# Down projection of the feed-forward stage by one level of Strassen's method over pairs of tiles, with weight sums and running sums on GpSimd

## The chip, the core and the metric

The kernel runs on one core of a Trainium2 chip. The metric is the device time of one execution in microseconds. Engines are named as in the profile: PE (TensorE), DVE (VectorE), ACT (ScalarE), POOL (GpSimd), SP (the engine that issues the DMAs).

## The reference, cut to what matters

One step of a two-layer encoder on 512 prompt frames and 8 × 16 sample frames. Each layer ends with a gated feed-forward stage, which is where the change lies:

```python
def swiglu(h, w_gu, w_down):
    g, u = jnp.split(h @ w_gu, 2, axis=-1)
    return (jax.nn.silu(g) * u) @ w_down
...
x = x + swiglu(rmsnorm(x, g_ffn[i]), w_ffn_gu[i], w_ffn_down[i])
```

The width is 1024 and the hidden width 2816, which is 22 tiles of 128. The 640 rows (512 prompt, 128 sample) are five tiles.

## The kernel before, in words

All products are float32 in three passes: a factor is held as a high part (rounded to the format that PE takes) and a low part (the rest), and hi·hi, hi·lo and lo·hi are added up in PSUM. So each weight goes through a **split**: ACT rounds it into `whi`, and DVE subtracts, `wlo = raw - whi`, with both inputs in SBUF (L1090, L1091 in `split_pair`). There are three buffers each of `whi` and `wlo`, 1024 columns wide.

The feed-forward stage works on pairs of hidden tiles, `g` = 0 to 10. `gate_up(g)` makes the gate and then the up projection, each by Winograd's form of Strassen's method: seven products of 12 matmuls over 320 columns, where plain products would need eight. For them `weights` forms four sums of weight blocks (`tw`, L1105 to L1108, one buffer, on DVE), and DVE adds each product from PSUM into results (L1133). `up` multiplies with the gate (L1170), and `finish` splits the activations into `aT` (L1055 on ACT, L1056 on DVE), in four pieces of 320 columns as they come.

`down` is plain before the change: after the gate of every even `g`, the two finished pairs g-2 and g-1 are multiplied with their rows of the down weight: 10 outputs of 128 rows by 512 columns, 12 matmuls of 512 columns each, and each is added from PSUM to the residual `X` by `add_x` (L318, DVE). So one **period** of the stage, over two pairs, holds two gates, two ups and one down. Each layer has five periods; the pair g = 10 is left for a last down, tile by tile, before the next norm.

The order of each engine's instructions is fixed when the program is built, by a scheduler that starts from the order in the code. Each engine works through its own list in order. Five PSUM banks serve these products (three `mm`, two `ps_s`).

Of the kernel before, what the change touches and what calls it, by code (L numbers as in the profile page):

```python
# [18 lines left out]
P = 128  # L19
# [73 lines left out]
def fox_mla_kernel(ctx: ExitStack, tc: tile.TileContext, I, O):  # L93
# [906 lines left out]
    def ffn_phase(l, nx, rest, g_next, cls=None):  # L1000
# [4 lines left out]

        w_gu, w_dn = I["w_ffn_gu"][l], I["w_ffn_down"][l]
# [3 lines left out]
        H0, H1 = slice(0, HALF), slice(HALF, NT)  # L1010
        with tc.tile_pool(name=f"ffn{l}", bufs=2, reuse_waits="tile") as fp:
# [33 lines left out]
            def alloc(g):  # L1045
                t = fp.tile([P, 2, 2, NT], F32R, tag="big", name="aT", bufs=2)
                aTs[g] = [t[:, 0], t[:, 1]]
# [4 lines left out]
            def finish(g, j, r):  # L1052

                a, (hi, lo) = avs[g], aTs[g]
                A.copy(hi[:, j, r], a[:, j, r])  # L1055
                V.tensor_tensor(lo[:, j, r], a[:, j, r], hi[:, j, r].bitcast(F32), ALU.subtract)  # L1056

            def plain(g):
# [3 lines left out]
                for n in range(2):  # L1062
# [6 lines left out]
                    def done(ps, j, hs, n=n):  # L1069
                        if n == 0:  # L1070
                            A.activation(a[:, j, hs], ps[:, 0:HALF], AF.Silu)
                        else:
                            V.tensor_tensor(a[:, j, hs], ps[:, 0:HALF], a[:, j, hs], ALU.mult)
                            finish(g, j, hs)
# [7 lines left out]
                return [lambda: alloc(g)] + L  # L1082
# [12 lines left out]
            def weights(c0):  # L1095
# [24 lines left out]
            def winograd(c0, out):  # L1120
# [19 lines left out]
                def p6(ps):  # L1140
                    d["u2"] = add(tmp("u2"), ps, "p1")
# [7 lines left out]
                def p5(ps):  # L1149
                    out(1, H1, add(tmp("c", 2), ps, "u3"))  # L1150
                    d["u4"] = add(tmp("u4"), ps, "u2")
# [11 lines left out]
            def gate_up(g):  # L1163
                a = avs[g] = a_tile()

                def gate(j, r, src):
                    A.activation(a[:, j, r], src, AF.Silu)

                def up(j, r, src):
                    V.tensor_tensor(a[:, j, r], src, a[:, j, r], ALU.mult)  # L1170
                    finish(g, j, r)

                return winograd(g * P, gate), [lambda: alloc(g)] + winograd(DFF + g * P, up)

            def down(gs):
# [3 lines left out]
                def load(half, g):  # L1179
# [3 lines left out]
                    d[half, g] = split_pair((raw, 2 * W))  # L1183

                def tile_half(t, half):
                    ac = slice(t * P, (t + 1) * P)

                    def ops():
                        return [(aTs[g][ai][:, j, ac], d[half, g][j][wi]) for g in gs for j in range(2) for wi, ai in PASSES]
                    return gemm(ops, 512, lambda ps: add_x(t, half, ps))  # L1190

                return load, tile_half

# [7 lines left out]
            for g in range(1, NG):  # L1201
                gate, up = gate_up(g)
                run(gate)
                if g % 2 == 0:
                    load, tile_half = down([g - 2, g - 1])
                    for half in range(2):
                        load(half, g - 2)
                        load(half, g - 1)
                        for t in range(TT):
                            run(tile_half(t, half))  # L1210
                run(up)
            load, tile_half = down([NG - 1])
            load(0, NG - 1)
            load(1, NG - 1)
# [523 lines left out]
```

## Time and profile before

| | us |
|---|---|
| runs: median of 3 | 2128.96 |
| runs: lowest, highest | 2126.95, 2131.17 |
| profiled execution, its own time | 2136.22 |
| span of the profile (first to last instruction) | 2134.4 |
| PE busy | 2071.8 |
| DVE busy | 1394.1 |
| ACT busy | 900.2 |
| POOL busy | 176.0 |

The profile is one execution, 7.26 us above the median of the runs; 1.8 us of its time lie outside the span. Busy time is a union over the whole span, so a low share does not say that an engine is idle in every stage.

### The profile page before, as it was taken

Reading aid. Unit: us, or ns where it says so; the run is one execution under the profiler, and the core shown is the slowest. Engines: PE = TensorE matmul, PEld = TensorE weight load, DVE = VectorE, ACT = ScalarE, POOL = GpSimd, SP = SyncE. Lnnn points to the kernel's source line nnn. Section 1 sums busy time; section 2 is a strip of 40 time slices with the busy share of each in tenths; the row PEclk is TensorE's granted clock in tenths of the full one; section 3 lists DMA queues with packets and bytes.
Section 4 is the critical chain, followed back from the end, with each engine's and each line's share of the span. In section 5 each row is a group of like instructions: output and inputs, shape, how many; then the busy total and the mean of one; then the engine's idle time right before and its main releaser. Section 6 shows DMA issues by size and latency. Waiting matters only on the chain. (4 is left out here: it accounts for less than half of the span.)

```text
span 2134.4 us, 35883 instructions
## 1 busy us (share of the span) xinstructions
PE 2071.8 (97%) x14189; PEld 1863.8 (87%) x14189; DVE 1394.1 (65%) x2695; ACT 900.2 (42%) x1793; POOL 176.0 (8%) x362
## 2 busy tenths in 40 slices
PE   7999999999999999999999999999999999999998
PEld 7988888888987799999998878887887799999997
DVE  4454555554546796696687567767546796686686
ACT  4444444454443443343344455554443443343342
POOL 1221212120100000000002201100000000000000
PEclk9999999999999999999999999999999999999999
DMA  7443434477545322232222221112445322322221
GB/s 222 130 137 108 140 108 128 149 233 226 161 142 184 96 73 80 89 90 79 80 80 59 84 92 39 52 50 87 141 145 182 99 70 79 89 87 77 84 80 59
DMA packets 279280, 234.34 MB, mean 110 GB/s; under 512 B 15669, under 2 KB 255925, under 8 KB 279113
## 3 DMA queue, kind: packets, MB, share of 16 engines
q1 hardware_dynamic: 279112, 232.05, 35.6%
q8 instruction: 112, 1.84, 0.4%
q14 instruction: 56, 0.45, 0.1%
HBM read 214.80 MB, written 17.21 MB: 109 GB/s over the span
## 5 line engine op out<-in xcount | busy, mean ns | idle before, releaser
L204 PE MATMUL mm<-hT,whi 128*128 128x320 f32 x1744 | 293.1, 314 | 4.3 <-ACT hT L222 4.3
L204 PEld LDWEIGHTS mm<-hT,whi 128*128 128x128 f32 x1744 | 262.6, 189 | 12.0 <-ACT hT L222 5.7
L318 DVE TENSOR_TENSOR X<-mm,X 128x512 f32<-128x512 f32 x270 | 182.8, 687 | 118.2 <-PE mm L204 116.7
L151 DVE TENSOR_TENSOR wlo<-raw,whi 128x1024 fp32r<-128x1024 f32 (+4 forms) x145 | 170.2, 1176 | 137.0 <-ACT whi L150 102.7
L150 ACT CAST whi<-raw 128x1024 fp32r<-128x1024 f32 (+4 forms) x145 | 144.7, 1002 | 162.5 <-PE mm L204 105.8
L204 PE MATMUL mm<-whi,oT 128*128 128x512 f32 x544 | 184.4, 411 | 1.3 <-DVE X L318 0.7
L1090 ACT CAST whi<-tw 128x512 fp32r<-128x512 f32 (+1 forms) x120 | 91.9, 766 | 213.0 <-PE mm L204 127.2
L204 PE MATMUL mm<-whi,aT 128*128 128x512 f32 x560 | 173.0, 390 | 0.3 <-ACT aT L1055 0.3
L204 PE MATMUL mm<-hT,wlo 128*128 128x320 f32 x872 | 156.7, 312 | 0.0
L204 PEld LDWEIGHTS mm<-hT,wlo 128*128 128x128 f32 x872 | 133.3, 188 | 3.2 <-issue 3.1
L204 PE MATMUL mm<-whi,hT 128*128 128x256 f32 (+2 forms) x800 | 127.5, 298 | 5.0 <-ACT whi L150 4.0
L204 PE MATMUL mm<-s,whi 128*128 128x320 f32 x768 | 128.2, 309 | 0.0
L204 PEld LDWEIGHTS mm<-whi,aT 128*128 128x128 f32 x560 | 104.4, 188 | 22.4 <-ACT aT L1055 1.1
L232 POOL TENSOR_SCALAR rstd<-ss 128x1 f32<-128x1 f32 x49 | 16.6, 339 | 1282.3 <-ACT hn L230 1277.8
L204 PEld LDWEIGHTS mm<-whi,hT 128*128 128x128 f32 x800 | 110.0, 193 | 10.3 <-ACT whi L150 4.5
L204 PEld LDWEIGHTS mm<-whi,oT 128*128 128x128 f32 x544 | 97.5, 190 | 22.7 <-issue 3.7
L204 PEld LDWEIGHTS mm<-s,whi 128*128 128x128 f32 x768 | 116.6, 188 | 0.0
L1091 DVE TENSOR_TENSOR wlo<-tw,whi 128x512 fp32r<-128x512 f32 (+1 forms) x120 | 103.5, 863 | 18.9 <-ACT whi L1090 16.7
L204 PE MATMUL mm<-wlo,oT 128*128 128x512 f32 x272 | 109.2, 402 | 0.0
L204 PE MATMUL mm<-wlo,aT 128*128 128x512 f32 x280 | 108.8, 389 | 0.0
L1090 ACT CAST whi<-raw 128x1024 fp32r<-128x1024 f32 x44 | 46.3, 1052 | 131.8 <-PE mm L204 72.3
L204 PE MATMUL ps_s<-whi,aT 128*128 128x512 f32 x320 | 98.6, 389 | 0.0
(340 smaller groups left out, 4289.0 us busy)
## 6 DMA issues: line engine op xcount, KB each, us to landing
rawg<-w_ffn_gu SPq DMA_DIRECT2D x80, 512.0 KB
raw<-w_ffn_down SPq DMA_DIRECT2D x44, 512.0 KB
raw<-w_x_kv SPq DMA_DIRECT2D x32, 512.0 KB
kr<-cache_mem_k SPq DMA_DIRECT2D x64, 256.0 KB
vr<-cache_mem_v SPq DMA_DIRECT2D x32, 512.0 KB
raw<-w_fox_in SPq DMA_DIRECT2D x30, 512.0 KB
kr<-cache_fox_k SPq DMA_DIRECT2D x16, 512.0 KB
vr<-cache_fox_v SPq DMA_DIRECT2D x16, 512.0 KB
```

The costliest lines, as they stand in the source:

```text
L150: A.copy(hi[:, 0:m], raw[:, 0:m])
L151: V.tensor_tensor(lo[:, 0:m], raw[:, 0:m], hi[:, 0:m].bitcast(F32), ALU.subtract)
L204: T.matmul(st["ps"][:, 0:n], lhsT=l, rhs=r, start=(j == 0), stop=(j == m - 1))
L232: G.tensor_scalar(r, ss, EPS, None, ALU.add)
L318: V.tensor_tensor(xs, ps, xs, ALU.add)
L1090: A.copy(hi[:, o:o + m], src)
L1091: V.tensor_tensor(lo[:, o:o + m], src, hi[:, o:o + m].bitcast(F32), ALU.subtract)
```

## The change

The four prompt tiles of the down projection become a Winograd product too (`down_winograd`): rows in two halves, columns in two halves, hidden tiles g-2 and g-1 as the blocks' inner parts. Seven products of 2 × 6 matmuls replace eight of the same size; the sample tile stays plain. `finish` runs once at the end of `up` and, except for the last pair, also forms and splits three sums of activations (256 columns each). The four sums of down-weight blocks (1024 columns) are taken on GpSimd in place in the loaded buffers, and all eight blocks are split, where four splits did before. Products that go into several outputs are first gathered in `u`, and GpSimd adds `u` to `X` (`spread`); the others are added by `add_x`. The four sums `tw` in `weights` go from DVE to GpSimd.

```diff
-                V.tensor_tensor(t[:, 2], b12, b11, ALU.subtract)
-                V.tensor_tensor(t[:, 0], b22, t[:, 2], ALU.subtract)
-                V.tensor_tensor(t[:, 1], b22, b12, ALU.subtract)
-                V.tensor_tensor(t[:, 3], b21, t[:, 0], ALU.subtract)
+                G.tensor_tensor(t[:, 2], b12, b11, ALU.subtract)
+                G.tensor_tensor(t[:, 0], b22, t[:, 2], ALU.subtract)
+                G.tensor_tensor(t[:, 1], b22, b12, ALU.subtract)
+                G.tensor_tensor(t[:, 3], b21, t[:, 0], ALU.subtract)
...
-            def finish(g, j, r):
-
-                a, (hi, lo) = avs[g], aTs[g]
-                A.copy(hi[:, j, r], a[:, j, r])
-                V.tensor_tensor(lo[:, j, r], a[:, j, r], hi[:, j, r].bitcast(F32), ALU.subtract)
+            def finish(g):
...
+                def split(c, src):
+                    A.copy(t[:, 0, c], src)
+                    V.tensor_tensor(t[:, 1, c], src, t[:, 0, c].bitcast(F32), ALU.subtract)
+
+                if g < NG - 1:
+                    a11, a12, a21, a22 = a[:, 0, R0], a[:, 1, R0], a[:, 0, R1], a[:, 1, R1]
+                    st = fp.tile([P, 3, NP // 2], F32, tag="u", name="st", bufs=2)
+                    V.tensor_tensor(st[:, 0], a21, a22, ALU.add)
+                    V.tensor_tensor(st[:, 1], st[:, 0], a11, ALU.subtract)
+                    V.tensor_tensor(st[:, 2], a12, st[:, 1], ALU.subtract)
+                    V.tensor_tensor(a21, a11, a21, ALU.subtract)
+                split(slice(0, M), a.rearrange("p j n -> p (j n)"))
+                if g < NG - 1:
+                    split(slice(M, M + 3 * NP // 2), st.rearrange("p j n -> p (j n)"))
...
+            def down_winograd(g0):
...
+                def sub(dst, x, y):
+                    G.tensor_tensor(d[dst], d[x], d[y], ALU.subtract)
...
+                def spread(i, *at):
+                    for r, half in at:
+                        G.tensor_tensor(xs(r, half, i), u[i], xs(r, half, i), ALU.add)
+
+                def p1(ps, i):
+                    u[i] = fp.tile([P, 512], F32, tag="u", name="u", bufs=2)
+                    A.copy(u[i], ps)
+                    spread(i, (0, 0))
+
+                def p6(ps, i):
+                    V.tensor_tensor(u[i], ps, u[i], ALU.add)
+                    spread(i, (0, 1))
+
+                def p7(ps, i):
+                    V.tensor_tensor(u[i], ps, u[i], ALU.add)
+                    spread(i, (1, 0), (1, 1))
...
+                def s1():
+                    split("b11", 0, 0)
+                    sub((0, 0), (0, 1), (0, 0))
+                    split("b21", 1, 0)
+                    both("b11", "11", p1)
+                    product("b11", 0, "s", 0, stop=False)
+
+                def s2():
+                    split("t1", 0, 0)
+                    sub((0, 0), (1, 1), (0, 0))
+                    sub((1, 0), (1, 0), (0, 0))
+                    product("b21", 1, "s", 0, start=False)
+                    add_x(TT - 1, 0, acc["s", 0])
+                    both("b21", "12", into((0, 0)))
+
+                def s3():
+                    split("b12", 0, 1)
+                    sub((0, 1), (1, 1), (0, 1))
+                    both("t1", "s1", into((0, 1), (1, 1)))
+
+                def s4():
+                    split("t2", 0, 0)
+                    product("b12", 0, "s", 0, stop=False)
+
+                def s5():
+                    split("b22", 1, 1)
+                    product("b22", 1, "s", 0, start=False)
+                    add_x(TT - 1, 1, acc["s", 0])
+                    both("b22", "s4", into((0, 1)))
...
+                def s8():
+                    both("t4", "22", into((1, 0)))
```

**POOL's list around a down.** Before, POOL has nothing to do in the whole feed-forward stage of layer 0 between one sum at its start (`s31`) and the small steps of the norm at its end (`rstd`):

```order
L232 TENSOR_SCALAR rstd_8811<-ss_8809 128x1
L233 TENSOR_TENSOR rstd_8811<-rstd_8811,mhalf_82 128x1
L1029 TENSOR_TENSOR s31_8933<-stmp_8930,s30_8932 128x1280
L232 TENSOR_SCALAR rstd_12830<-ss_12828 128x1
L233 TENSOR_TENSOR rstd_12830<-rstd_12830,mhalf_82 128x1
L232 TENSOR_SCALAR rstd_12853<-ss_12851 128x1
```

After, this stands in POOL's list around the first down of layer 0. `tw` are the sums for an up projection, `raw` and `rawd` the loaded down weights, `u` the two gathered products (9562 for the first tile of a row half, 9572 for the second):

```order
L1133 TENSOR_TENSOR tw_9739<-rawg_9735,tw_9739 128x512
L1236 TENSOR_TENSOR raw_9402<-rawd_9404,raw_9402 128x1024
L1236 TENSOR_TENSOR raw_9402<-rawd_9408,raw_9402 128x1024
L1259 TENSOR_TENSOR X_84<-u_9562,X_84 128x512
L1236 TENSOR_TENSOR raw_9406<-raw_9406,raw_9402 128x1024
L1259 TENSOR_TENSOR X_84<-u_9572,X_84 128x512
L1236 TENSOR_TENSOR rawd_9404<-rawd_9408,rawd_9404 128x1024
L1259 TENSOR_TENSOR X_84<-u_9562,X_84 128x512
L1259 TENSOR_TENSOR X_84<-u_9572,X_84 128x512
L1259 TENSOR_TENSOR X_84<-u_9562,X_84 128x512 x2
L1259 TENSOR_TENSOR X_84<-u_9572,X_84 128x512 x2
```

So 12 instructions per down and 16 `tw` sums per period came to POOL; the first two additions of `u` to `X` stand behind and between sums of weights.

**DVE's list in the same down.** Before, DVE has two splits (`wlo`) and, one by one, the additions to `X`:

```order
L1091 TENSOR_TENSOR wlo_9551<-raw_9548,whi_9550 128x1024
L1133 TENSOR_TENSOR c_9539<-mm_9526,u3_9490 128x320
L1091 TENSOR_TENSOR wlo_9627<-raw_9624,whi_9626 128x1024
L318 TENSOR_TENSOR X_84<-ps_s_9554,X_84 128x512
L318 TENSOR_TENSOR X_84<-ps_s_9568,X_84 128x512
L318 TENSOR_TENSOR X_84<-mm_9582,X_84 128x512
L318 TENSOR_TENSOR X_84<-mm_9596,X_84 128x512
L1091 TENSOR_TENSOR wlo_9633<-raw_9630,whi_9632 128x1024
L318 TENSOR_TENSOR X_84<-mm_9610,X_84 128x512
```

After, DVE has this there; 9575 is the sample tile, 9595 and 9603 the two tiles of product b21, 9616 and 9625 those of t1, which go into two outputs each:

```order
L1116 TENSOR_TENSOR wlo_9583<-raw_9402,whi_9582 128x1024
L1116 TENSOR_TENSOR wlo_9612<-rawd_9404,whi_9611 128x1024
L318 TENSOR_TENSOR X_84<-mm_9575,X_84 128x512
L318 TENSOR_TENSOR X_84<-mm_9595,X_84 128x512
L318 TENSOR_TENSOR X_84<-mm_9603,X_84 128x512
L1116 TENSOR_TENSOR wlo_9635<-raw_9402,whi_9634 128x1024
L318 TENSOR_TENSOR X_84<-ps_s_9616,X_84 128x512 x2
L318 TENSOR_TENSOR X_84<-ps_s_9625,X_84 128x512 x2
L1116 TENSOR_TENSOR wlo_9646<-rawd_9408,whi_9645 128x1024
L1116 TENSOR_TENSOR wlo_9673<-rawd_9404,whi_9672 128x1024
```

Twice as many splits stand between the additions, and the addition of `mm_9603` has to come after POOL's addition of `u_9572` to the same part of `X`.

**DVE's list at the end of the layer**, where the last up is followed by the last down. Before, the pieces of `aT` stand between the last multiplications:

```order
L1056 TENSOR_TENSOR aT_12650<-a_12347,aT_12650 128x320
L1170 TENSOR_TENSOR a_12347<-c_12774,a_12347 128x320
L1133 TENSOR_TENSOR c_12792<-mm_12779,u3_12739 128x320
L151 TENSOR_TENSOR wlo_13029<-raw_13027,whi_13028 128x1008
L1056 TENSOR_TENSOR aT_12650<-a_12347,aT_12650 128x320
L1170 TENSOR_TENSOR a_12347<-c_12792,a_12347 128x320
L318 TENSOR_TENSOR X_84<-mm_12811,X_84 128x512
L1056 TENSOR_TENSOR aT_12650<-a_12347,aT_12650 128x320
```

After, one piece of 1280 columns follows the last multiplication, and no matmul of the last down can start ahead of its high part on ACT:

```order
L1116 TENSOR_TENSOR wlo_12930<-raw_12927,whi_12929 128x1024
L1195 TENSOR_TENSOR a_12449<-c_12900,a_12449 128x320
L1158 TENSOR_TENSOR c_12916<-mm_12903,u3_12868 128x320
L151 TENSOR_TENSOR wlo_13153<-raw_13151,whi_13152 128x1008
L1195 TENSOR_TENSOR a_12449<-c_12916,a_12449 128x320
L1063 TENSOR_TENSOR aT_12782<-a_12449,aT_12782 128x1280
L318 TENSOR_TENSOR X_84<-mm_12935,X_84 128x512
```

## Rows read from the trace of the kernel before

**Rows 1.** The page: busy time by engine; granted clock in 40 slices.

```profile
PE 2071.8 (97%) x14189; PEld 1863.8 (87%) x14189; DVE 1394.1 (65%) x2695; ACT 900.2 (42%) x1793; POOL 176.0 (8%) x362
...
PEclk9999999999999999999999999999999999999999
```

**Rows 2.** Windows: one down; the two ups and gates behind it.

```profile
803.60:830.80 27.20, 27.20 (x122) 22.54 (x121) 10.69 (x15) 4.58 (x5) 0.00 (x0) 1.00 0.24 78
830.80:880.10 49.30, 49.30 (x337) 49.26 (x337) 45.40 (x81) 23.73 (x39) 0.00 (x0) 1.00 0.29 86
```

**Rows 3.** PE timeline, first and last of two runs: start, us.

```profile
770.18 1.34 PE L204 MATMUL ps_s<-s,whi 128*128 128x320 f32 x8
...
801.86 1.34 PE L204 MATMUL mm<-hT,whi 128*128 128x320 f32 x8
...
804.31 0.63 PE L204 MATMUL ps_s<-whi,aT 128*128 128x512 f32 x2
...
830.16 0.62 PE L204 MATMUL mm<-whi,aT 128*128 128x512 f32 x2
```

**Rows 4.** DVE timeline, two places without gaps between instructions.

```profile
831.69 0.68 DVE L318 TENSOR_TENSOR X<-mm,X 128x512 f32<-128x512 f32 x1
832.29 0.68 DVE L1091 TENSOR_TENSOR wlo<-tw,whi 128x512 fp32r<-128x512 f32 x1
832.89 0.68 DVE L1091 TENSOR_TENSOR wlo<-rawg,whi 128x512 fp32r<-128x512 f32 x1
...
839.69 1.22 DVE L1091 TENSOR_TENSOR wlo<-rawg,whi 128x1024 fp32r<-128x1024 f32 x1
840.82 0.48 DVE L1133 TENSOR_TENSOR c<-mm,u 128x320 f32<-128x320 f32 x1
841.22 0.48 DVE L1133 TENSOR_TENSOR u<-mm,u 128x320 f32<-128x320 f32 x1
```

**Rows 5.** Groups of DVE by form, one period, 831 to 907.5 us.

```profile
L318 DVE TENSOR_TENSOR X<-mm,X 128x512 f32<-128x512 f32 x6 | 4.1, 689 | 4.4 <-PE mm L204 4.3
L1056 DVE TENSOR_TENSOR aT<-a,aT 128x320 fp32r<-128x320 f32 x8 | 3.9, 486 | 0.0
...
L1105 DVE TENSOR_TENSOR tw<-rawg 128x512 f32<-128x512 f32 x4 | 2.7, 683 | 0.0
```

**Rows 6.** Lines with sums on POOL: ns of one, min/median/max.

```profile
L738 POOL TENSOR_TENSOR oT<-sig,oT x8: 1561/1715/1862, 115.6 to 514.3; 128x640 fp32r<-128x640 f32 x8
...
L1029 POOL TENSOR_TENSOR s<-stmp,s x2: 2978/2980/2983, 761.7 to 1721.7; 128x1280 fp32r<-128x1280 f32 x2
...
L1642 POOL TENSOR_TENSOR oT<-oTf,oT x7: 1276/1283/1474, 1284.9 to 1471.7; 128x512 fp32r<-128x512 f32 x7
```

**Rows 7.** Timelines of DVE and POOL, four places with both at work.

```profile
762.42 3.33 DVE L1091 TENSOR_TENSOR wlo<-rawg,whi 128x1024 fp32r<-128x1024 f32 x1
761.69 2.98 POOL L1029 TENSOR_TENSOR s<-stmp,s 128x1280 fp32r<-128x1280 f32 x1 [22.50 <-ACT s L1028]
...
114.62 1.23 DVE L151 TENSOR_TENSOR wlo<-raw,whi 128x1024 fp32r<-128x1024 f32 x1
115.56 1.72 POOL L738 TENSOR_TENSOR oT<-sig,oT 128x640 fp32r<-128x640 f32 x1 [5.82 <-ACT oT L737]
...
435.91 1.23 DVE L151 TENSOR_TENSOR wlo<-raw,whi 128x1024 fp32r<-128x1024 f32 x1 [0.45 <-ACT whi L150]
436.10 1.19 POOL L592 TENSOR_SCALAR_AFFINE_SELECT pw<-pw 128x128 f32<-128x128 f32 x1
...
390.73 0.69 DVE L318 TENSOR_TENSOR X<-mm,X 128x512 f32<-128x512 f32 x1
390.61 0.87 POOL L591 TENSOR_SCALAR pw<-ckb,cq 128x256 f32<-128x256 f32 x2
```

**Rows 8.** Timelines: ACT, 1280 columns; PE, last down of layer 0.

```profile
756.03 1.27 ACT L1028 CAST s<-big 128x1280 fp32r<-128x1280 f32 x1
...
1150.96 1.21 PE L204 MATMUL mm<-whi,aT 128*128 128x512 f32 x4 [0.25 <-ACT aT L1055]
```

More of the change, by code (lines that the diff above doesn't have):

```diff
@@ L1081, in plain @@
                                       lambda ps, j=j, hs=hs, done=done: done(ps, j, hs))
[L1082 removed]
+                return [lambda: alloc(g)] + L + [lambda: finish(g)]
             def split_pair(*srcs):
@@ L1190, in tile_half, with load, split, product @@
                     return gemm(ops, 512, lambda ps: add_x(t, half, ps))
                 return load, tile_half
+            def down_winograd(g0):
+                d, acc, u = {}, {}, {}
+                wv = w_dn.rearrange("(j g p) n -> j p g n", j=2, p=P)
+                def load():
+                    for j in range(2):
+                        for half in range(2):
+                            if half == 0:
+                                r = wpool.tile([P, UNIT], F32, tag="raw", name="raw", bufs=2)
+                            else:
+                                r = npool.tile([P, UNIT], F32, tag="hn", name="rawd", bufs=2)
+                            S.dma_start(r.rearrange("p (g n) -> p g n", g=2),
+                                        wv[j][:, g0:g0 + 2, half * 512:(half + 1) * 512])
+                            d[j, half] = r
+                def split(n, *at):
+                    d[n] = split_pair((d[at], 2 * W))
+                def sub(dst, x, y):
+                    G.tensor_tensor(d[dst], d[x], d[y], ALU.subtract)
+                def product(w, rows, n, i, start=True, stop=True):
+                    if start:
+                        acc[n, i] = psum_mm()
+                    m = 0
+                    for j in range(2):
+                        l = plain_op(g0 + j, rows, TT - 1) if isinstance(rows, int) else operand(g0 + j, rows, i)
+                        for wi, ai in PASSES:
+                            T.matmul(acc[n, i], lhsT=l[ai], rhs=d[w][j][wi], start=start and m == 0, stop=stop and m == 5)
+                            m += 1
+                def xs(r, half, i):
+                    return X[:, 2 * r + i, half * 512:(half + 1) * 512]
+                def both(w, rows, done):
+                    for i in range(2):
+                        product(w, rows, rows, i)
+                        done(acc[rows, i], i)
+                def spread(i, *at):
[11 more added lines that the diff above has]
+                    spread(i, (1, 0), (1, 1))
+                def into(*at):
+                    def done(ps, i):
+                        for r, half in at:
+                            add_x(2 * r + i, half, ps)
+                    return done
+                def s1():
[23 more added lines that the diff above has]
+                    both("b22", "s4", into((0, 1)))
+                def s6():
+                    split("t3", 0, 1)
+                    both("t2", "s2", p6)
+                def s7():
+                    split("t4", 1, 0)
+                    both("t3", "s3", p7)
+                def s8():
+                    both("t4", "22", into((1, 0)))
+                return load, [s1, s2, s3, s4, s5, s6, s7, s8]
@@ L1202, in ffn_phase @@
                 gate, up = gate_up(g)
+                if g % 2 == 0:
+                    load, steps = down_winograd(g - 2)
+                    load()
                 run(gate)
                 if g % 2 == 0:
[L1205 to L1210, printed above, removed]
+                    run(steps)
                 run(up)
-            load, tile_half = down([NG - 1])
-            load(0, NG - 1)
-            load(1, NG - 1)
+            load, tile_half = down(NG - 1)
+            load(0)
+            load(1)
             wide[0] = False
```

28 lines of the change are left out of this document (16 added, 12 removed).

## The prediction

> **What bounds the kernel now.** I read the page first: PE is busy for 97% of the span, at the full granted clock [rows 1]. The windows say the same of the stage that is changed: in one down and the four projections behind it PE has no idle time, 27.2 + 49.3 = 76.5 us for a period [rows 2]. So PE's columns are the bound, and a matmul left out is time won, as long as nobody makes PE wait. The second column to read there is DVE: 45.4 of 49.3 us in gates and ups, 10.7 of 27.2 in the down [rows 2]. In gates and ups DVE is nearly a second bound; the down is where it rests.
>
> **What PE saves.** From the first to the last row of the projections 18 products of 12 matmuls take 31.68 us, 146.7 ns for a matmul of 320 columns; in the down 38 groups of three take 25.85 us, 226.7 ns for 512 columns [rows 3]. The down goes from 120 matmuls to 7 × 12 + 24 for the sample tile = 108: 24.5 us instead of 27.2, -2.7 us a period, **-27 us** for the ten periods. If nothing else held PE, a period would take 73.8 us.
>
> **DVE by itself.** I take the distance from start to start, since neighbours overlap a little: 0.60 us for 512 columns (from SBUF or PSUM), 1.13 for 1024, 0.40 for 320 [rows 4]; between them 1.035 ns a column, which gives 1.40 for 1280, 0.87 for 768 and 0.34 for 256.
> Gates and ups of a period, after: 8 splits of 1024 (9.0), 12 of 512 (7.2), 8 multiplications (3.2), two times `finish` with four sums, a 1280 and a 768 (7.2), 28 additions from PSUM (11.2): 37.8 us. Gone are the 16 `tw` sums (four rows like the one shown) and the eight pieces of `aT` [rows 5].
> The down: 8 splits (9.0) and 16 additions from PSUM (12 to `X`, 4 to `u`; 9.6): 18.6 us, where ten additions [rows 5] (the row has the six that come from `mm` banks) and four splits stood. Together 56.4 us of 73.8: alone, DVE fits.
> ACT gains four roundings of 1024, two of 768 and two copies of `u`, some 6 us on 28.3 a period [rows 2]: it stays under half. `finish` is late by design, but the down reads it only a gate later (12.3 us); without that cover it would show, as it does at the end (below).
>
> **POOL.** 512 columns of a sum with two inputs take 1.28 us (the least of seven), 1280 take 2.98 [rows 6]; a straight line gives 2.41 for 1024. Per period: 16 `tw` and 8 additions to `X` of 1.28, 4 sums of 2.41, 40.4 us. POOL alone fits too.
>
> **What the two do to each other.** This decides. At 762.42 a split of 1024 columns took 3.33 us instead of 1.22: POOL was in a sum of two SBUF inputs from 761.69 to 764.67, and the split ended 1.08 us after that [rows 7, 4]. The other way round, POOL's product at 115.56 took 1.72 us, where it takes 1.56 at its least; the split ahead of it ended at 115.85, so POOL ended 1.43 us after DVE [rows 6, 7]. At 436.10 POOL again comes behind a split (435.91 to 437.14) and ends at 437.29 [rows 7]. So a DVE instruction with two SBUF inputs and a POOL one that reads SBUF run one after the other, whichever is first. An addition with one input in PSUM is free of it: 0.69 us at 390.73, in the middle of POOL's 390.61 to 391.48 [rows 7]. Some 0.13 us at the start of the one that waits is hidden (1.56 - 1.43).
> So a turn of POOL costs DVE 1.28 - 0.13 = 1.15 us, or 2.28 for 1024 columns, less what DVE can do meanwhile from PSUM. All splits, multiplications and `finish` have two SBUF inputs.
> Gates and ups: 37.8 + 16 × 1.15 = 56.2 us with nothing covered, against PE's 49.3. On DVE's list 28 PSUM additions lie among 40 others, 0.7 × 0.40 = 0.28 us to a turn: 4.5 us covered, 51.7.
> The down: 18.6 + 8 × 1.15 + 4 × 2.28 = 36.9, against PE's 24.5. Six of the 16 PSUM additions (two tiles each of b21, p7 and t4) wait for POOL themselves and cannot run under it, so I take half of 9.6 as covered: 32.1.
> Sum 83.8 us. I take off half of the 3.9 us in which DVE now idles in gates and ups [rows 2], where a turn costs nothing: **82 us** a period against 76.5, +5.5, and **+55 us** for ten, PE's saving already in it. Bounds: all PSUM work covered, and PE is the bound again, 73.8; nothing covered, 56.2 + 36.9 = 93.1, or +166 us in ten periods. Break-even of the total is 75.8, with 17.3 of the 20.8 us of PSUM work covered.
>
> The Trainium skill has this as a rule (SBUF — State Buffer, "Who interferes with whom"): a VectorE instruction with two SBUF inputs and a GpSimd instruction that reads SBUF exclude each other, and the second to issue is blocked until the first is done. By the rows the start of the blocked one is hidden, 0.13 us; with whole instructions as the page has it, the turns would come to 40.4 us a period instead of 36.7, and the forecast to some 37 us more.
>
> **Where it stalls.** In the down, DVE's addition of `mm_9603` needs POOL's addition of `u_9572`, which stands in POOL's list behind two sums of 2.41 us, the addition of `u_9562` and a third sum; the splits t2 and b22, four additions to `X` and the PSUM banks of `mm` wait behind it on DVE. The second sum cannot start before the split of t1, itself made from the first sum. From the split of b11 the chain is 2.41 (first sum) + 1.0 (ACT, by its 1.27 for 1280 columns [rows 8]) + 1.13 + 2.41 + 1.28 + 2.41 + 1.28 = 11.9 us. b11's buffer is that of t2 and t3 of the gate, free after four of its seven products, 5.3 us ahead of the down; the split takes 2.1, so the chain ends 8.7 us into the down, and PE has ended product b21 at 8.2 (36 × 0.227). Then DVE has the addition, the split t2, four additions and the split b22, 0.6 + 1.1 + 2.4 + 1.1: 13.9 us, and PE wants the low part of b22 at its 63rd matmul, 14.3. So no slack is left, and a turn lost in this chain is PE's. It is part of the 82, not added to it.
>
> **Ends of the layers.** The last down follows the last up at once. Before, PE waited 0.25 us there, for one piece of `aT` [rows 8], and a few tenths more. After: addition 0.40, a split of the next phase 1.13, multiplication 0.40, ACT's 1280 columns 1.27 [rows 8], the low part 1.40, less three matmuls in between: some 4 us, so 3.5 more, **+7 us** for two layers.
>
> **Sum.** 55 + 7 = +62: the profiled execution of 2136.2 us (span 2134.4 and 1.8 around it) would be 2198. It lay 7.3 above the median of the runs, so I forecast **2191 us** for the median.
>
> **Rivals.**
> - *POOL's turns are covered* (faster): the scheduler's order puts them under PSUM additions and idle time, and PE keeps its gain: -27 + 7, 2109 us. It decides from 17.3 us covered. For it: DVE had 16.5 us idle in the down before. Against: POOL's work and DVE's with two SBUF inputs come to 40.4 + 35.6 = 76 us a period, and 73.8 are there, so even the hidden starts would be needed.
> - *Only the chain in the down costs*: one long turn (2.28 us) is lost in it a period, and gates and ups lose nothing: -27 + 23 + 7 = +3, no change, 2132 us. For it: the chain has no slack. Against: in gates and ups the sum without cover is 6.9 us over PE's time, so cover would have to be nearly whole there.
> - *Little is covered*: PSUM additions come in runs when a product ends, and while DVE waits for a turn PE gets no weights, so that both are late together. Halfway between my 82 and 93.1, 87.5 us a period: +110 + 7, 2246 us.
> - *Whole instructions are excluded*: by 3.7 us a period more than in the sum, 2228 us. The rows show the hidden start only for a waiting instruction that was already issued. The skill's page named above states it so.
>
> **Chances.** Forecast (some 79 to 85 us a period) 0.62; covered 0.13; only the chain 0.06; little covered 0.11; whole instructions 0.08. A difference of 0.2% (4 us) is about what can be told from no change. Faster: 0.14 (the covered case and a good end of the forecast's); same: 0.06; slower: 0.80. The range leaves out the core of the covered case and the far half of the last but one: 2122 to 2275. The forecast's own range, 79 to 85, is 2161 to 2221.
>
> **What would show each step.** PE's 512-column matmuls in the down at 227 ns, 108 of them, with idle time between; that idle ended by DVE (`wlo`) above all. Splits of 1024 columns at 2 to 3.5 us where POOL works, and POOL's 512-column sums at a mean well over 1.28; additions from PSUM unchanged at 0.69. DVE busy over 90% in the stage. A period of 80 to 85 us in the windows. Wrong would be: splits that stay at 1.22 us beside a busy POOL, or PE without idle time at 73.8 us a period.

## The result and the profile after

The changed kernel takes 2232.7 us (median of 4 runs, 2230.1 to 2236.1). The kernel before took 2130.1 us on the same chip (4 runs, 2127.0 to 2132.6). The ratio is 1.048, with a 95% interval of 1.0462 to 1.0497: 103 us slower. The forecast was 2191 us, with a range of 2122 to 2275: the direction was right, the size 42 us short, and the time is above the forecast's own range of 2161 to 2221.

The page of the changed kernel, busy time by engine and the granted clock in 40 slices, answers to [rows 1]:

```profile
PE 2098.5 (94%) x14069; PEld 1863.6 (83%) x14069; DVE 1536.5 (69%) x2669; ACT 945.4 (42%) x1807; POOL 697.8 (31%) x642
...
PEclk9999999999999999999999999999999999999998
```

PE has 120 matmuls less, twelve in each of ten downs, as forecast, and is busy longer all the same. The slices are too coarse to show why; the windows do, here the two ups and gates ahead of a down, that down, and a part of it (length, then busy time and count of PE, PEld, DVE, ACT and POOL, PE's granted clock, DMA's share and rate):

```profile
840.70:890.60 49.90, 49.82 (x338) 49.29 (x337) 43.35 (x65) 21.21 (x32) 30.93 (x19) 1.00 0.27 81
890.70:926.50 35.80, 29.08 (x109) 22.00 (x109) 26.70 (x29) 11.54 (x15) 21.43 (x12) 0.86 0.20 68
908.70:919.00 10.30, 6.92 (x16) 4.96 (x16) 7.48 (x9) 1.22 (x2) 0.36 (x1) 0.50 0.43 152
```

From first matmul to first matmul gates and ups went from 49.3 to 49.8 us, the down from 27.2 [rows 2] to 35.9. So almost the whole loss lies in the down, and for 10.3 us of it PE's clock is at its lower level, 1.2 GHz. PE's timeline of this down, the waits and a stretch behind them:

```profile
892.37 0.51 PE L1246 MATMUL mm<-wlo,aT 128*128 128x512 f32 x1 [1.04 <-DVE wlo L1116]
...
907.53 0.73 PE L1246 MATMUL mm<-whi,aT 128*128 128x512 f32 x2 [1.65 <-DVE X L318]
911.39 1.22 PE L1246 MATMUL mm<-whi,aT 128*128 128x512 f32 x2 [3.13 <-DVE X L318]
...
913.72 0.80 PE L1246 MATMUL ps_s<-wlo,aT 128*128 128x512 f32 x1 [0.68 <-DVE wlo L1116]
...
916.02 1.05 PE L1246 MATMUL mm<-whi,aT 128*128 128x512 f32 x2
916.88 1.05 PE L1246 MATMUL mm<-wlo,aT 128*128 128x512 f32 x2
...
926.52 1.33 PE L204 MATMUL ps_s<-hT,whi 128*128 128x320 f32 x8
```

With one of 0.22 us that is not shown, the waits come to 6.7 us, and each costs about 0.27 us beyond its idle time (a row is 0.39 us long where the pace is 0.227, and the first matmul behind a wait is 0.11 slower). At 916.02 two matmuls of 512 columns take 0.86 us, 0.43 each, where they take 0.227 at full clock [rows 3]; the window at 0.50 holds 16 of them, which makes 3.2 us lost. 24.5 + 6.7 + 1.4 + 3.2 = 35.8. What PE waits for in the middle is one addition on DVE, then those behind the next split, and DVE waits for POOL. Timelines of DVE and POOL, from ahead of the down, which starts at 890.66, to that place:

```profile
885.78 2.33 DVE L1063 TENSOR_TENSOR aT<-a,aT 128x1280 fp32r<-128x1280 f32 x1
888.03 2.04 DVE L1063 TENSOR_TENSOR aT<-st,aT 128x768 fp32r<-128x768 f32 x1
...
890.40 1.91 DVE L1116 TENSOR_TENSOR wlo<-raw,whi 128x1024 fp32r<-128x1024 f32 x1
...
899.76 2.25 DVE L1116 TENSOR_TENSOR wlo<-rawd,whi 128x1024 fp32r<-128x1024 f32 x1 [1.31 <-ACT whi L1115]
...
906.78 0.69 DVE L318 TENSOR_TENSOR X<-mm,X 128x512 f32<-128x512 f32 x1 [2.90 <-POOL X L1259]
907.39 2.75 DVE L1116 TENSOR_TENSOR wlo<-raw,whi 128x1024 fp32r<-128x1024 f32 x1
910.07 1.27 DVE L318 TENSOR_TENSOR X<-mm,X 128x512 f32<-128x512 f32 x2
```

```profile
893.43 2.40 POOL L1236 TENSOR_TENSOR raw<-rawd,raw 128x1024 f32<-128x1024 f32 x1
898.52 2.40 POOL L1236 TENSOR_TENSOR raw<-rawd,raw 128x1024 f32<-128x1024 f32 x1 [2.69 <-DVE wlo L1116]
900.88 2.29 POOL L1259 TENSOR_TENSOR X<-u,X 128x512 f32<-128x512 f32 x1
903.12 2.40 POOL L1236 TENSOR_TENSOR raw<-raw 128x1024 f32<-128x1024 f32 x1
905.49 1.27 POOL L1259 TENSOR_TENSOR X<-u,X 128x512 f32<-128x512 f32 x1
906.71 2.35 POOL L1236 TENSOR_TENSOR rawd<-rawd 128x1024 f32<-128x1024 f32 x1
```

The second addition of the first product (905.49), whose `u` ScalarE had copied by 898.78, stands behind two weight sums. It ends at 906.76, and DVE's addition starts. Then the split of t2 takes 2.75 us, since POOL is already in the next sum, and PE's banks stay taken for as long.

Two places outside the downs are slower too. At the start of a layer's stage the transposes wait for DVE (PE, DVE and POOL timelines of the changed kernel, rows of each, then DVE's in the kernel before):

```profile
746.01 1.11 PE L246 MATMUL ps_t<-cst,hn 128*128 128x128 f32 x4 [4.15 <-DVE hT L223]
...
738.07 5.08 DVE L1026 TENSOR_TENSOR big<-hT,hT 128x1280 f32<-128x1280 f32 x2
...
739.26 2.54 POOL L1131 TENSOR_TENSOR tw<-rawg,tw 128x512 f32<-128x512 f32 x1
...
740.43 2.88 DVE L1023 TENSOR_TENSOR big<-hT,hT 128x1280 f32<-128x1280 f32 x2
```

Two sums of 1280 columns took 2.88 us together before; next to POOL's first `tw` sums they take 5.08. At the end of a layer the last down waits for `aT` in one piece, 4.55 us in layer 0 and 2.67 in layer 1 (PE timeline):

```profile
1199.95 2.32 PE L204 MATMUL mm<-whi,aT 128*128 128x512 f32 x4 [4.55 <-ACT aT L1062]
```

The profiled executions differ by 99.9 us. The ten downs of pairs have 80 of it (they take 33.5 to 35.9 us, 35.3 on average), the gates and ups between them 4, and the ends 13 (4.7 and 2.8 us ahead of the last downs, which themselves take 11.3 and 17.6 us for 9.1 and 14.1). The starts have 10, 6.4 us in layer 0 and 3.9 in layer 1: the longer wait and matmuls at the lower clock behind it. The rest of the program, which the change does not touch, was 8 shorter.

### The profile page after: what moved, and what is told of

Its sections match the earlier page's. It is cut to its first block, busy times and chain, and to the rows that moved or that the text cites. A ratio compares the mean times of both kernels' runs of the same rounds, so it can differ in the third digit from the quotient of the medians.

```text
span 2234.3 us, 36173 instructions
## 1 busy us (share of the span) xinstructions
PE 2098.5 (94%) x14069; PEld 1863.6 (83%) x14069; DVE 1536.5 (69%) x2669; ACT 945.4 (42%) x1807; POOL 697.8 (31%) x642
## 3 DMA queue, kind: packets, MB, share of 16 engines
q8 instruction: 111, 1.82, 0.3%
## 4 chain that ended last, share of the span: by engine, by line
PE 58%; DVE 16%; POOL 13%; ACT 4%; issue 4%; DMA 4%; SPq 0%; DVEq 0%; POOLq 0%; ACTq 0%
PE mm L204 34%; DVE wlo L1116 6%; PE mm L1246 3%; POOL raw L1236 3%; POOL tw L1132 3%; PE ps_s L218 2%; POOL tw L1131 2%; PE ps_s L1246 2%; DMA kr<-cache_mem_k 2%; POOL tw L1130 2%; POOL X L1259 2%; PE ps_s L204 2%; DVE X L318 1%; PE ps_t L913 1%; ACT whi L1115 1%
## 5 line engine op out<-in xcount | busy, mean ns | idle before, releaser
L318 DVE TENSOR_TENSOR X<-mm,X 128x512 f32<-128x512 f32 x282 | 189.3, 685 | 101.4 <-PE mm L204 51.4
L1259 POOL TENSOR_TENSOR X<-u,X 128x512 f32<-128x512 f32 x80 | 140.1, 1776 | 113.7 <-DVE u L1267 113.7
L1246 PE MATMUL mm<-whi,aT 128*128 128x512 f32 x432 | 144.5, 419 | 28.7 <-DVE X L318 28.7
L1116 DVE TENSOR_TENSOR wlo<-tw,whi 128x512 fp32r<-128x512 f32 (+1 forms) x120 | 115.2, 960 | 38.2 <-ACT whi L1115 38.2
L1246 PEld LDWEIGHTS mm<-whi,aT 128*128 128x128 f32 x432 | 86.3, 203 | 51.1 <-DVE X L318 33.8
L591 POOL TENSOR_SCALAR pw<-ckb,cq 128x256 f32<-128x256 f32 (+2 forms) x64 | 40.6, 639 | 260.3 <-PE ps_t L623 142.6
L1130 POOL TENSOR_TENSOR tw<-rawg 128x512 f32<-128x512 f32 x40 | 54.8, 1369 | 190.4 <-DVE wlo L1116 176.6
```

Source lines behind the costliest of these rows:

```text
L318: V.tensor_tensor(xs, ps, xs, ALU.add)
L1116: V.tensor_tensor(lo[:, o:o + m], src, hi[:, o:o + m].bitcast(F32), ALU.subtract)
L1130: G.tensor_tensor(t[:, 2], b12, b11, ALU.subtract)
L1246: T.matmul(acc[n, i], lhsT=l[ai], rhs=d[w][j][wi], start=start and m == 0, stop=stop and m == 5)
L1259: G.tensor_tensor(xs(r, half, i), u[i], xs(r, half, i), ALU.add)
```

## The experiments

The theory to be tested: GpSimd's turns make VectorE late, by exclusion and by the order of GpSimd's list; TensorE waits; and its clock falls behind the wait. The rivals are the doubled splits themselves, GpSimd's slowness without any exclusion, and the 16 `tw` sums of a period as the main cost.

**Only the `tw` sums on GpSimd.** The kernel before, with one edit:

```
-                V.tensor_tensor(t[:, 2], b12, b11, ALU.subtract)     (and three more)
+                G.tensor_tensor(t[:, 2], b12, b11, ALU.subtract)
```

> The kernel before, with its 16 tw sums a period on GpSimd and nothing else changed. Theory (the two engines shut each other out, and in the down GpSimd's list makes VectorE late): gates and ups keep up, 49.3 to 49.9 us a period, the down stays at 27.2: 2130 to 2138 us. Rival (the tw sums cost most, since they are 20 of the 40 us on GpSimd): half or more of the loss, 2180 us or above. VectorE's splits of 1024 columns beside a busy GpSimd should be longer than 1.22 us by either.

Measured: 2139.2 us against 2128.7, 1.0054 [1.0035, 1.0074], 1 us above the theory's range. Down and gates and ups are as before, 27.2 and 49.3; the sums take 1.38 to 1.82 us on average, by line. What is lost lies at the starts of the stages, where PE waits 4.15 us for `hT` in layer 0. So 16 turns a period cost PE nothing while DVE has room, and the third rival is out: by themselves these sums are not the main cost. In the changed kernel they do make `finish` late, as shown below.

**The down's sums and additions on VectorE,** the `tw` sums still on GpSimd:

```
-                    G.tensor_tensor(d[dst], d[x], d[y], ALU.subtract)
+                    V.tensor_tensor(d[dst], d[x], d[y], ALU.subtract)
-                        G.tensor_tensor(xs(r, half, i), u[i], xs(r, half, i), ALU.add)
+                        V.tensor_tensor(xs(r, half, i), u[i], xs(r, half, i), ALU.add)
```

> The changed kernel with the down's four weight sums and eight additions of u on VectorE; the tw sums stay on GpSimd. VectorE gets some 9 us more work in each down. Theory (exclusion and GpSimd's list): without them the down takes VectorE's own 28 to 30 us instead of 35.7, and 2155 to 2180 us in all. Rival (the doubled splits and the other added work on VectorE and ScalarE make the down late, wherever the sums run): the down grows to 40 us or more, 2270 us or above.

Measured: 2175.4, 1.0226 [1.0205, 1.0247], inside the theory's range. Downs take 27.8 to 31.3 us in place of 33.5 to 35.9 (in four of the ten the clock falls, for 3.4 us), though DVE's list there is 9.3 us longer (4 × 1.13 + 8 × 0.60). The doubled splits are not the main cost.

**GpSimd busy as long, but only writing:**

```
-                    G.tensor_tensor(d[dst], d[x], d[y], ALU.subtract)
+                    G.memset(d[dst], 0.01)
+                    G.memset(d[dst], 0.01)
+                    G.memset(d[dst][:, 0:512], 0.01)     (and three in place of each tw sum)
```

> The changed kernel with each weight sum on GpSimd (16 tw sums and four sums of down weights a period) replaced by three writes of a constant that take GpSimd about as long and read nothing; the products are then of other weights. The eight additions of u stay. Theory (exclusion): splits of 1024 columns go back to about 1.22 us outside the additions, the down takes 27 to 31 us, 2150 to 2190 us in all. Rival (GpSimd is only slow, its latency holds the chain; exclusion does not matter): nothing changes, 2225 to 2240 us.

Measured: 2109.0, 0.9916 [0.9889, 0.9942], the fastest of all, but its products use other weights, so it is no kernel to take. A down takes 24.5 us, gates and ups 49.3, with PE busy throughout; that is the 73.8 us that the prediction gave as the period without any hold-up. Splits are at their shortest beside POOL's writes (DVE, then POOL):

```profile
880.06 1.23 DVE L1116 TENSOR_TENSOR wlo<-raw,whi 128x1024 fp32r<-128x1024 f32 x1 [0.16 <-ACT whi L1115]
...
879.46 0.95 POOL L1245 MEMSET rawd<- 128x1024 f32 x1
880.47 0.53 POOL L1246 MEMSET rawd<- 128x512 f32 x1
```

The expectation of 27 to 31 us, and 2150 in all, was too high: without reads of SBUF in the 20 sums, the eight additions alone cost PE nothing. But exclusion is not the only thing that is gone. The scheduler put the first two additions between the short writes, at 873.13 and 875.73, 2.4 and 5.0 us into the down, where they start 10.2 and 14.8 us into it in the changed kernel. So this run does not part exclusion from the order of POOL's list; the next one and the last one do. The Trainium skill (SBUF — State Buffer, "Who interferes with whom") says that VectorE's second SBUF input contends with a GpSimd instruction that reads SBUF, not with one that only writes; the trace agrees, 1.23 us here where the same split, that of t2, took 2.75 at 907.39 in the changed kernel.

**The first product straight from PSUM.** Two of GpSimd's instructions a down are taken out of its list:

```
                     A.copy(u[i], ps)
-                    spread(i, (0, 0))
+                    add_x(i, 0, ps)
```

> The changed kernel with the first product added to X by VectorE from PSUM, not by GpSimd from u: two instructions less on GpSimd a down, two of 0.6 us more on VectorE. Theory (GpSimd's list: additions to X behind weight sums hold VectorE, which holds the PSUM banks): VectorE's wait of up to 2.9 us for GpSimd goes, and with it TensorE's longest wait of 3.1 us and the low clock behind it; down 30 to 33 us, 2185 to 2215 us. Rival (only the sum of turns counts): two turns less, 2 us a down at most, and the clock still falls: 2212 to 2232 us.

Measured: 2165.9, 1.0178 [1.0159, 1.0197], better than expected. Windows of gates and ups, and of a down:

```profile
831.20:880.90 49.70, 49.69 (x337) 49.18 (x335) 43.13 (x65) 21.20 (x32) 30.74 (x18) 1.00 0.27 79
881.00:909.60 28.60, 25.72 (x109) 19.98 (x109) 26.59 (x31) 11.56 (x15) 19.91 (x10) 1.00 0.27 84
```

POOL is busy in the down for 19.9 us, hardly less than 21.4, and DVE for as long as in the changed kernel. Only PE's waits of 1.65, 3.13 and 0.68 us have shrunk, to 0.25 and 1.36, and with them, in nine of ten downs, the low clock is gone. A down takes 28.7 us, less than the 30 to 33 expected. Two instructions were worth some 64 us (1.048 to 1.0178).

**Everything on VectorE:** the edits of the second run, and the `tw` sums back on VectorE.

> All sums and additions on VectorE, nothing of the change on GpSimd; products, order and ends of a layer as in the changed kernel. Exclusion theory: no turns are left, so every weight split takes 1.22 us and every addition about 0.61 to 0.68; VectorE's work of a period comes to 75 to 76 us, of which the down's part is 12 instructions of 1.22 and 24 of 0.61, 29.3 us. The period is 75 to 77 us against 76.5 before, the gap at the start of a layer's stage is gone, and the ends still cost about 7: 2115 to 2145 us. Rival, the new structure itself (eight splits and seven products with ScalarE and VectorE in line) holds TensorE up, wherever the sums run: the down stays at 33 us or more, 2180 us or more.

Measured: 2163.3, 1.0158 [1.0138, 1.0178]. The rival is out, but the expectation is missed by 18 us. The downs take 24.5 to 25.6 us, and gates and ups 54.0 on average: DVE works through its list of the down into the next projection, whose `tw` sums stand behind it, and PE waits there once a period; behind that wait its clock is at 0.50 for 3.4 us or more in nine of the ten periods (DVE timeline, then PE's):

```profile
901.56 1.28 DVE L318 TENSOR_TENSOR X<-mm,X 128x512 f32<-128x512 f32 x2
902.76 0.68 DVE L1131 TENSOR_TENSOR tw<-rawg,tw 128x512 f32<-128x512 f32 x1
...
905.25 1.48 PE L204 MATMUL mm<-s,whi 128*128 128x320 f32 x5 [2.93 <-ACT whi L1115]
```

DVE is busy for 76.2 of the 79.4 us of this period. So alone DVE is nearly the bound. That is 69 us faster than the changed kernel, and still 33 slower than the kernel before.

**The two edges of a stage,** in the changed kernel:

```
+                E = V if c0 == P else G
-                G.tensor_tensor(t[:, 2], b12, b11, ALU.subtract)     (and three more)
+                E.tensor_tensor(t[:, 2], b12, b11, ALU.subtract)
...
                     V.tensor_tensor(a[:, j, r], src, a[:, j, r], ALU.mult)
+                    if g == NG - 1:
+                        piece(g, j, r)     (one ACT copy and one subtraction of a[:, j, r], as before)
```

> The changed kernel with two edits at the edges of a layer's stage: the four sums of weights of the first gate on VectorE, and the last pair of tiles split in four pieces as each is ready, as before the change. If the start of the stage is late because VectorE's sums of the first operands and GpSimd's sums of weights wait for each other, the gap of TensorE there shrinks from 7.9 to about 3.4 us in each layer (-9 in all); the pieces take TensorE's gap ahead of the last down from 4.5 and 2.7 us to below 1.5 and shorten that down by 2 to 3 (-7 to -9 in all). Together 2214 to 2222 us against 2232.7. If the delay only moves on, to the first gates or the norm behind the last down, 2228 to 2236. The periods between stay at 85.6 us in either case.

Measured: 2212.4, 1.0385 [1.0369, 1.0400], 20.3 below the changed kernel and a little better than expected. The wait of 4.15 us is gone, that ahead of the last down of layer 0 is 1.20 for 4.55, and that down takes 10.0 for 11.3. Downs and gates between are as in the changed kernel, 35.8 and 49.8 in the windows that answer to those above.

**Sums on VectorE, additions on GpSimd.** Both edges, the first product from PSUM, and the weight sums of the down on VectorE (three edits shown above).

> The two edits at the edges, and in the down: the four weight sums on VectorE, the first product added to X from PSUM by VectorE, six additions of running sums to X left on GpSimd, behind the sixth and seventh product. Exclusion theory, with a price for each turn: VectorE has 12 instructions of 1.22 and 18 of 0.61 us in a down, 25.6 us, and GpSimd's six turns fall to the end of the down and into the next gates, where VectorE has room: down 26 to 28, gates and ups 49.9, the granted clock at full speed in the downs; 2120 to 2150 us. If the additions on GpSimd cost as much as the sums did (each a wait of TensorE, whatever its place), the down stays at 30 or more and the time at 2160 or more.

Measured: 2160.6, 1.0141 [1.0126, 1.0156], above the theory's range and at the lower edge of the other's. Eight of its ten downs come in two lengths, 29.5 and 31.0 us, four of each, with the same four waits of PE to 0.05 us (one has a fifth, of 0.28). Windows of one of each and of a stretch in the second, then waits of PE in the second:

```profile
878.30:907.70 29.40, 25.83 (x109) 19.85 (x109) 29.01 (x35) 10.52 (x13) 7.41 (x5) 1.00 0.21 72
957.70:988.70 31.00, 27.43 (x110) 21.11 (x109) 29.25 (x35) 10.52 (x13) 7.46 (x5) 0.94 0.20 68
...
977.00:980.40 3.40, 3.40 (x10) 2.66 (x9) 2.42 (x3) 0.00 (x0) 0.00 (x0) 0.50 0.70 213
```

```profile
974.28 0.74 PE L1256 MATMUL mm<-whi,aT 128*128 128x512 f32 x2 [0.46 <-DVE X L318]
976.61 0.51 PE L1256 MATMUL mm<-wlo,aT 128*128 128x512 f32 x1 [1.59 <-DVE wlo L1122]
```

In the first they are 0.46 and 1.59 too, at 894.82 and 897.15. Behind them the clock stays full once and falls to 0.50 the other time, and that alone is 1.6 us.

The two waits are not the additions' doing. The run with the additions on VectorE too has them as well (PE timeline of the second experiment):

```profile
898.74 0.73 PE L1246 MATMUL mm<-whi,aT 128*128 128x512 f32 x2 [0.46 <-DVE X L318]
901.06 0.50 PE L1246 MATMUL mm<-wlo,aT 128*128 128x512 f32 x1 [1.60 <-DVE wlo L1116]
```

So it makes no difference to these waits whether the additions behind the sixth and seventh product are on GpSimd. What both runs share is the four weight sums in VectorE's list, and that list is full: DVE is busy for 29.0 of the 29.4 us of the first window, more than the 25.6 that were expected.

**Four additions on GpSimd in place of six:** the sixth product's two go to VectorE.

```
-                    spread(i, (0, 1))
+                    spread(i, (0, 1), E=V)
```

> As the run with six additions on GpSimd, but the two additions of the sixth product's running sum on VectorE too; four additions stay on GpSimd, at the very end of the down. VectorE has 12 instructions of 1.22 and 20 of 0.61 us, 26.8 us, and two turns fewer. If a turn costs VectorE more than the addition itself (0.61 us), this is the faster of the two by up to 1 us a period, 10 us in all: 2115 to 2145. If the turns lie beside idle time of VectorE, it is the slower one by up to 12 us.

Measured: 2165.4, 1.0161 [1.0144, 1.0178]; the intervals of the two runs overlap. PE's four waits in a down are the same, gates and ups take 50.2 us for 50.0, and the clock fell in seven downs for five. So the first expectation is out; that it is slower because the turns lie beside idle time of DVE is not shown.

**The joined kernel, with late sums:** first product from PSUM, both edges, and in the program

```
-                    sub((1, 0), (1, 0), (0, 0))     (from s2; and the sum for t3, from s3)
                     split("b22", 1, 1)
+                    sub((0, 1), (1, 1), (0, 1))
+                    sub((1, 0), (1, 0), (0, 0))
```

> The run with the first product added from PSUM, with the two edits at the edges, and the sums for t3 and t4 on GpSimd moved behind the split of b22 in the program. Without the move, the two runs that it joins give 2165.9 - 20.3 = 2145.6 us. In the run with the first product added from PSUM TensorE waits in a down 1.04 us for b21's split, 0.23 and 0.25 in between, and 1.36 us for b22's split, which came behind the GpSimd sums of t2 and t4 (2.3 us for the second of VectorE's splits in place of 1.2). Exclusion theory: the move takes the last two of these waits away, 1.4 to 2 us in each of 10 downs, with the rate after it some 2: down 26.5 to 27.5 against 28.8, 2125 to 2138 us. If the sums only block other splits behind them (t3's own, and then the last product waits for it), the down stays at 28.5 to 29.5 and the time at 2142 to 2152.

Measured: 2145.7, 1.0063 [1.0039, 1.0087]. The move did nothing: GpSimd's list in a down is t1, t2, t4, t3 as without it, since the scheduler sets the order and not the line in the program. So the late sums stay untried, and that the time lies in the second range says nothing for that theory. What the run does show is that the two gains add up, as in the sum of 2145.6 above.

**The next up's `tw` sums on VectorE,** called between s6 and s7, on top of it:

```
-                E = V if c0 == P else G
+                E = V if c0 == P or c0 >= DFF and (c0 - DFF) // P % 2 == 0 else G
...
-                    run(steps)
+                    run(steps[:6])
+                    run(up[1:2])     (the loads and the four sums of the up)
+                    run(steps[6:])
```

> As the run with the late sums, and the weight sums of the up that follows a down on VectorE (four of 0.61 us in place of four turns of GpSimd that fall beside the splits of the activations and of b11 and b21), and the additions to X's quarter (1, 1) on GpSimd behind those to (1, 0). If a turn costs VectorE more than the sum itself, the wait of 1.04 us at the start of a down goes as well: down 25 to 26.5 and 2115 to 2130 us, some 10 below the run with the late sums. If the sums on VectorE only take their place in its queue, ahead of the same splits, the down is the same within 0.5 us and so is the time within 6 us.

Measured: 2173.3, 1.0193 [1.0164, 1.0223], 28 us slower than without it, which neither theory had. The wait of 1.04 us at the start of a down is gone, as the first theory had it. But the scheduler put the four sums among the first splits of the down, and there they meet the long sums on POOL (DVE timeline, then POOL's):

```profile
881.24 2.71 DVE L1137 TENSOR_TENSOR tw<-rawg 128x512 f32<-128x512 f32 x1
...
888.94 2.51 DVE L1139 TENSOR_TENSOR tw<-rawg 128x512 f32<-128x512 f32 x1
...
881.00 2.40 POOL L1250 TENSOR_TENSOR raw<-rawd,raw 128x1024 f32<-128x1024 f32 x1 [9.93 <-DVE wlo L1122]
888.50 2.41 POOL L1250 TENSOR_TENSOR raw<-rawd,raw 128x1024 f32<-128x1024 f32 x1 [5.09 <-DVE wlo L1122]
```

An instruction of 0.6 us on DVE costs 2.5 when it comes behind a turn of 2.4. In the down shown PE waits 2.38 and 1.07 us for the additions behind them, and the clock falls in nine of the ten downs.

**And the sixth product's additions on VectorE.**

> As the run with the up's sums on VectorE, with the two additions of the sixth product's running sum on VectorE too (0.61 us each), which leaves four additions and four sums on GpSimd in a down. VectorE has 1 to 2 us of idle time in the down's last third in the run with the first product added from PSUM, and waits there 1.85 us for GpSimd's last additions. If that idle time takes the two additions, the last wait shrinks and the time is up to 5 us less than with six on GpSimd; if VectorE's list of the down is full again once the waits are gone, it is 5 to 15 us more.

Measured: 2173.9, 1.0206 [1.0176, 1.0235], no difference. Nothing follows from it, since the down was already late where the edit acts.

**One operand of the splits in PSUM.** On the joined kernel, the down's split:

```
                     A.copy(hi, d[at])
+                    for h in range(2):
+                        c, ph = slice(h * W, (h + 1) * W), psum_t()
+                        A.copy(ph, hi[:, c].bitcast(F32))
-                    V.tensor_tensor(lo, d[at], hi.bitcast(F32), ALU.subtract)
+                        V.tensor_tensor(lo[:, c], d[at][:, c], ph, ALU.subtract)
```

> As the run with the late sums (its order on GpSimd came out as without the move: t1, t2, t4, t3), but each weight split of the down takes ScalarE's high part from PSUM: ScalarE writes it to SBUF for TensorE as before and a second time, in two halves, to PSUM, and VectorE subtracts there in two halves of 512. All values are the same. Only the operands' place changes for VectorE, which then has one input in SBUF and not two. Exclusion theory: the eight splits of a down no longer take turns with GpSimd's sums; two halves take 1.27 to 1.4 us each time, against 1.2 to 2.3, GpSimd's sums stay at 2.4, and the waits of TensorE in a down (1.04, 0.2, 0.3 and 1.4 us) go, but for ScalarE's second copy (1.1 us later) where a split is not ready ahead: down 25.5 to 27.5 against 28.8, 2112 to 2135 us. If GpSimd holds VectorE up wherever the operand is, or the wait is for GpSimd's sums as data, the down stays at 28.5 to 30 and the time at 2143 to 2160.

Measured: 2130.4 (11 runs) against 2129.0 (15 runs), 1.0005 [0.9994, 1.0017], some 12 us below the joined kernel (1.0063 to 1.0005): no slower than the kernel before and no faster, and the best of the changed kernels that compute the reference. Timelines of DVE and POOL in a down, and the windows of gates and ups and of that down:

```profile
889.35 1.28 DVE L1249 TENSOR_TENSOR wlo<-rawd,ps_t 128x512 fp32r<-128x512 f32 x2
...
892.95 0.68 DVE L1249 TENSOR_TENSOR wlo<-raw,ps_t 128x512 fp32r<-128x512 f32 x1
...
888.21 2.41 POOL L1253 TENSOR_TENSOR raw<-rawd,raw 128x1024 f32<-128x1024 f32 x1 [3.92 <-DVE wlo L1249]
890.70 2.42 POOL L1253 TENSOR_TENSOR raw<-raw 128x1024 f32<-128x1024 f32 x1
893.06 2.41 POOL L1253 TENSOR_TENSOR rawd<-rawd 128x1024 f32<-128x1024 f32 x1
```

```profile
830.10:879.40 49.30, 49.30 (x338) 49.22 (x336) 43.27 (x65) 22.32 (x34) 30.36 (x18) 1.00 0.29 85
879.40:907.20 27.80, 25.67 (x109) 20.00 (x109) 23.52 (x39) 18.95 (x28) 16.85 (x10) 1.00 0.24 77
```

POOL's sums run through at 2.41 us, in the same order as in the joined kernel, and DVE's splits beside them at 0.68 a half. The turns are gone where only one input is in SBUF, and the same section of the Trainium skill says so of a VectorE instruction with at most one SBUF input, outside modes that use two ports; the trace agrees. In place of 28.7 us the down takes 27.9, and gates and ups 49.3 for 49.8. So to take the down's eight splits out of the turns is worth some 12 us, what ScalarE's second copies cost already taken off. The time is inside the range of the exclusion theory, the down is not, 27.9 us and not 25.5 to 27.5: DVE now waits 0.70 and 1.06 us for ScalarE's second copy, and PE has waits of 0.39, 0.43, 0.63 and 0.68 us.

## Why the prediction was right in direction and short in size

- **PE's saving**, -2.7 us a period: right. With nothing in the way (the run with writes only) a period is 73.8 us, to the tenth.
- **Exclusion and its price**: right. In the changed kernel a split beside POOL's sum ended 1.09 us after it (899.76, 2.25 us long; the sum ended at 900.92), so 0.13 us is hidden, as worked out from [rows 7]. Additions from PSUM stayed at 0.69. The rival with whole instructions gave 2228, near to the time measured, but for a reason that this row speaks against.
- **Gates and ups, 51.7**: measured 49.8. DVE is busy there for 43.4 us where 56.2 would be busy with nothing covered, so some 13 us are covered and not 4.5, by this estimate, and PE stays the bound. That the 1.9 us taken off in the 82 lead to the measured time is luck.
- **The down, 32.1**: measured 35.3 on average, and this is the term that was mis-sized, by some 31 us in ten downs. TensorE at its lower level behind its own waits is most of it: 13 to 16 matmuls in each of the ten downs at 0.43 us for 0.227, 2.6 to 3.2 us a down and some 30 in all. By this estimate, which takes every other wait as it is, the down shown would take 32.7 at full clock. The prediction read the full clock in [rows 1] and kept it for a kernel that waits. That the low clock costs time by itself is shown by the run with two lengths of down, 1.6 us there with fewer matmuls at the low level. That 32.7 lies so near to 32.1 is luck: 32.1 was DVE's own work with its turns, and DVE was busy for only 26.7 of the 35.8 us.
- **The chain in the down**: its place and its parts were right, its start was not. It was to begin with a split of b11 that ends 3.2 us ahead of the down; DVE ended that at 892.3, 1.65 us into it, since `finish` of the pair stood ahead of it and met POOL's `tw` sums (2.33 and 2.04 us, where beside POOL's writes they take 1.49 and 0.95), and the first weight sum came behind those at 893.43. So the addition of `mm_9603` stood at 16.1 us of the down, not at 8.7. It and the split and additions behind it have 4.8 of the 6.7 us of waits. The run without the two additions on GpSimd shows it.
- **The ends, +7**: measured 13. The waits, 7.2 together, are the forecast's; the last downs then run at the low clock behind them, which was left out.
- **The starts**: left out, 10 us in both layers together. The sums of the first operands on DVE and POOL's first `tw` sums exclude each other by the rule that the prediction had, at a place that it did not go through.
- **DVE busy over 90% in the stage**: wrong, 43.4 of 49.9 us and 26.7 of 35.8. DVE waited for POOL's list, 2.90 us at a time; it was late by order, not by load. In this the truth lies between the forecast and the rival by which only the chain costs: gates and ups lost 0.5 us, but the chain cost more than twice the 2.28 of that rival. The rival with little cover, 87.5 us a period, is nearer to the 85.6 of the period shown than the forecast's 82, but not by its mechanism: in gates and ups more was covered than forecast, not less.

What stays open: whether t3's and t4's sums behind b22's split would help, since the order could not be moved by moving the lines, and why the clock falls behind the same waits in one down and not in the next.

## What to carry to other kernels

Work that is moved to GpSimd beside a VectorE with two SBUF inputs is not a second engine's time but time in turns: price it by what stands behind it in both lists, and first take out of GpSimd's list whatever VectorE waits for (some 64 us here). An operand that can be had from PSUM frees VectorE of the turns, at the price of a ScalarE copy (some 12 us won here). None of this made the change pay: the best of these kernels takes as long as the one before. Where a forecast makes TensorE wait, add a term for matmuls at 1.2 GHz behind the wait, and look through the starts and ends of stages as closely as their middle.

## What the hardware showed that was not expected

- The granted clock fell to 0.50 after TensorE had idled 0.46 and then 1.59 us, in four of the eight downs with these waits (31.0 us for 29.5). In the changed kernel it fell in every down of a pair, for 6.8 to 10.3 us, in which a matmul of 512 columns took 0.43 us.
- GpSimd's writes alone (0.95 us for 1024 columns) leave VectorE's splits at 1.23 us, and splits with one input in PSUM run at 0.68 a half beside GpSimd's sums of 2.41.
